# Two more input pairs transposed on VectorE in a matmul with rotary embedding

## The chip, the cores and the metric

The kernel runs on one core of a Trainium2 chip. The metric is the device time of one execution, in microseconds (us), as the median of several runs.

The core has five engines with a queue of instructions each: TensorE (PE in the profile; its weight loads are PEld), VectorE (DVE), ScalarE (ACT), GpSimd (POOL) and SyncE (SP). They run beside one another and wait for each other through semaphores. Here SP issues nearly all loads, ScalarE most stores, and GpSimd the loads of five pairs.

## The reference

```python
def reference(x, weight, cos, sin, n_heads):
    batch, seq, hidden = x.shape            # 16, 512, 768
    head_dim = hidden // n_heads            # 12 heads of 64
    y = np.matmul(x, weight)                # weight 768 x 768, all float32
    y = y.reshape(batch, seq, n_heads, head_dim)
    y1, y2 = y[..., :32], y[..., 32:]
    ...
    out1 = y1 * cos1 - y2 * sin1
    out2 = y2 * cos2 + y1 * sin2
    out = np.concatenate([out1, out2], axis=-1)
    return out.reshape(batch, seq, hidden)
```

So 8192 rows of 768 numbers are multiplied by one 768 x 768 matrix, and the result is rotated head by head with a cosine and a sine that depend on the row's place in its sequence.

## The kernel before

The 8192 rows are cut into 64 halves of 128 rows; two halves (`s` = 0 and 1, of two neighbouring batches) make a pair, `n` = 0 to 31. A pair goes through these stages:

1. Load. The 128 x 768 float32 rows of a half come to SBUF.
2. Cast to FP16 (`cast`, on ScalarE except at the start).
3. Transpose. A matmul contracts over the partitions, so the rows must be turned until the 768 columns lie on partitions, in six pieces of 128 x 128.
4. Matmul (`mm`, line 174): for each of the six pieces the transposed rows are the stationary operand, and 768 columns of the weight stream past.
5. `rope` (line 188) on VectorE: one instruction multiplies a PSUM bank with cosine and with sine into `tq`. `add` (line 199) on GpSimd adds the two products, crosswise, into `ov`.
6. `store` (line 244).

There are three ways through stages 1 to 3.

- An ordinary pair: two loads by SP, one for each half, into the ten buffers of `xpool` (`load`, line 83); casts on ScalarE; six TensorE transposes into PSUM for each half (`transpose`, line 140); and a copy out of PSUM on ScalarE (line 76).
- A pair in `BLOCKS` (8, 12, 16, 20, 24): four quarter loads by GpSimd, which cast on the way (`load_blocks`); no cast on ScalarE; one VectorE block transpose for each half (`transpose_blocks`, line 148).
- A pair in `BLOCKS_SP` (10, 14, 18, 22, 26): four quarter loads by SP in float32 into one of the two buffers of `hpool` (`load_blocks_sp`, line 99); two casts on ScalarE; one VectorE block transpose for each half.

VectorE's block transpose turns only blocks of 32 x 32 in place. That is why such a pair is loaded in quarters: each quarter puts 192 of the 768 columns of all rows on 32 of the partitions, so that the blocks, once turned, make up whole pieces.

The order on every engine is the order in which the program is written. The main loop runs over `n`. At its head it issues loads for later pairs: `load_pair(n + 5)`, and the four quarters of pairs `n + 8`, `n + 7`, `n + 6` and `n + 5`. Then for each half it does the matmuls, the transposes of the next pair (`upto("turn", ...)`), the casts of the pair after that (`upto("cast", ...)`), and the rope of one or two PSUM banks. The store of pair `n - 3` stands at the end. The last four pairs (`ALONE`) are handled in half banks of 384 columns, so that work left at the end is short. Pairs 0 to 6 are loaded ahead of the loop.

In the built program SP's and ScalarE's DMAs take eight completion semaphores in turn, and a DMA waits at its issuer until the DMA that used the same semaphore last has landed. A wait at the head of a queue holds up all that is queued behind it.

Of the kernel before, what the change touches and what calls it, by code (L numbers as in the profile page):

```python
# [17 lines left out]
def kernel(  # L18
# [23 lines left out]
    AHEAD = 7  # L42
    AHEAD_B = 8
    ALONE = 4
    BLOCKS = range(8, 25, 4)
    BLOCKS_SP = range(10, 27, 4)

# [30 lines left out]
    def load(n, s):  # L80
        b, r = where(n, s)
        xss[n, s] = xpool.tile([P, H], FP32, tag="xs", name="xs")
        nc.sync.dma_start(  # L83
            out=xss[n, s], in_=x[b].rearrange("(p r) h -> r p h", r=SB)[r]
        )

    def load_pair(n):
        for s in (0, 1):
            if n < NP and n not in BLOCKS and n not in BLOCKS_SP:
                load(n, s)  # L90
# [4 lines left out]
    def load_quarter(n, q, eng, dst):  # L95
        b, r = where(n, 0)
        src = x[b : b + 2].rearrange("b (j a r) (q k) -> r q a (b j) k", r=SB, a=R, q=NQ)
        dst = dst.rearrange("p s (j k) -> p (s j) k", j=NQ)
        eng.dma_start(out=dst[ts(q, R)], in_=src[r, q])  # L99

    def load_blocks(n, quarters):
        if n not in BLOCKS:
            return
        if quarters[0] == 0:
            xhs[n] = bpool.tile([P, 2, H], FP16, tag="xh", name="xh")
            x16[n, 0], x16[n, 1] = xhs[n][:, 0], xhs[n][:, 1]
        for q in quarters:
            load_quarter(n, q, nc.gpsimd, xhs[n])

    def load_blocks_sp(n, q):  # L110
        if n not in BLOCKS_SP:
            return
        if q == 0:
            xhs[n] = hpool.tile([P, 2, H], FP32, tag="xf", name="xf")
            xss[n, 0], xss[n, 1] = xhs[n][:, 0], xhs[n][:, 1]
        load_quarter(n, q, nc.sync, xhs[n])
# [11 lines left out]
    def cast(n, s, eng):  # L128
        xc = cpool.tile([P, H], FP16, tag="xc", name="xc")
        x16[n, s] = xc  # L130
        src = xss.pop((n, s))
        src = src.rearrange("p (m t e) -> p t m e", t=NT, e=2)
        copy(eng, xc.rearrange("p (t m e) -> p t m e", t=NT, e=2), src)
# [11 lines left out]
    def transpose_blocks(n, s):  # L145
        order = "p (j a t) -> p t j a" if n in BLOCKS else "p (t j a) -> p t j a"
        xT = tpool.tile([P, NT, P, 2], FP16, tag="xT", name="xT")
        nc.vector.transpose(  # L148
            out=xT.bitcast(FP32).rearrange("p t (j a) o -> p t j (a o)", j=NQ),
            in_=x16.pop((n, s)).bitcast(FP32).rearrange(order, j=NQ, t=NT),  # L150
        )
        xTT[n, s] = xT.rearrange("p t m e -> p t e m")
# [4 lines left out]
    def psum(n, s):  # L157
        key, banks = (n, 3) if n < NP - ALONE else ((n, s), 2)
        if key not in psys:
            psys[key] = [  # L160
                py_pool.tile([P, 512], FP32, tag="psy", name="psy") for _ in range(banks)
            ]
        ps = psys[key]
        if banks == 2:
            return [(ps[k][:, 0:HH], k * HH, (k + 1) * HH) for k in (0, 1)]
        cut = 512 if s == 0 else 256
        return [(ps[s][:, ds(s * 256, cut)], 0, cut), (ps[s + 1][:, 0 : H - cut], cut, H)]

    def mm(n, s, t, e, c0=0, c1=H):
        for k, (ps, lo, hi) in enumerate(psum(n, s)):  # L170
            a, z = max(c0, lo), min(c1, hi)
            if a >= z:
                continue
            nc.tensor.matmul(  # L174
                ps[:, a - lo : z - lo],
                xTT[n, s][:, t, e, :],
                w_sb[:, t, e, a:z],
                start=((t, e) == CHUNKS[0] and n > 1),
                stop=((t, e) == CHUNKS[-1] and (n > 1 or s >= k)),
            )  # L180
# [15 lines left out]
    def add(n, c0, c1, eng):  # L196
        w = c1 - c0
        tq = tqs[n][:, :, ds(c0, w)]
        eng.tensor_tensor(  # L199
            out=ovs[n][:, ds(c0, w)].rearrange("p (h t d) -> p h t d", t=2, d=HD),  # L200
            in0=tq[:, 0].rearrange("p (h t d) -> p h t d", t=2, d=HD),
            in1=tq[:, 1].rearrange("p (h t d) -> p h t d", t=2, d=HD)[:, :, ::-1, :],
            op=ADD,
        )

    def rope_bank(n, b):
        rope(n, b * 512, (b + 1) * 512, psys[n][b])

    def add_pair(n, step=2 * H):
        for c in range(0, 2 * H, step):  # L210
            add(n, c, c + step, nc.gpsimd)
# [8 lines left out]
    def rope_last(n, ps, c0, c1):  # L220
        nh = (c1 - c0) // D
        q = tqs[n][:, 1, c0:c1]
        ph = ps.rearrange("p (h d) -> p h d", d=D)
        for o, j in ((q.rearrange("p (h d) -> p h d", d=D), 1), (ph, 0)):
            nc.vector.tensor_tensor(  # L225
                out=o, in0=ph, op=MULT,
                in1=csn[:, j, n % SB, :].unsqueeze(1).broadcast_to((P, nh, D)),
            )
        nc.vector.tensor_tensor(  # L229
            out=ovs[n][:, c0:c1].rearrange("p (h t d) -> p h t d", t=2, d=HD),  # L230
            in0=ps.rearrange("p (h t d) -> p h t d", t=2, d=HD),
            in1=q.rearrange("p (h t d) -> p h t d", t=2, d=HD)[:, :, ::-1, :],
            op=ADD,
        )

    def store(n, eng, c0=0, c1=2 * H):
        b, r = where(n, 0)
        dst = out.rearrange("b (p r) h -> r p b h", r=SB)[r, :, b : b + 2]
        src = ovs[n].rearrange("p (b h) -> p b h", b=2)
        if c1 - c0 < 2 * H:  # L240
            s = c0 // H
            dst = dst[:, s, c0 - s * H : c1 - s * H]
            src = src[:, s, c0 - s * H : c1 - s * H]
        eng.dma_start(out=dst, in_=src)
# [32 lines left out]
        load_w(t, e)  # L277
    nc.sync.dma_start(out=csn[:, 0], in_=cos.rearrange("(p r) d -> p r d", r=SB))
    nc.sync.dma_start(out=sin_sb, in_=sin.rearrange("(p r) d -> p r d", r=SB))
    for n in range(2, AHEAD):  # L280
        load_pair(n)


    done = {"cast": 4, "turn": 4}

    def upto(what, k):
        while done[what] < min(k, 2 * NP):
            n, s = divmod(done[what], 2)
            done[what] += 1
            if what == "cast":  # L290
                if n not in BLOCKS:
                    cast(n, s, nc.scalar)
            elif n in BLOCKS or n in BLOCKS_SP:
                transpose_blocks(n, s)
            else:
                transpose(n, s, nc.scalar)
# [46 lines left out]
    for n in range(2, NP):  # L343
        load_pair(n + AHEAD - 2)
        for q, ahead in ((0, 8), (2, 7), (1, 6), (3, 5)):
            load_blocks_sp(n + ahead, q)
        for m, quarters in ((n + AHEAD_B, (0, 2)), (n + AHEAD_B - 1, (1, 3))):
            if m > BLOCKS[0]:
                load_blocks(m, quarters)
        for s in (0, 1):  # L350
            i = 2 * n + s
            if n < 4:

                for c0, c1 in ((0, 256), (256, H)):
                    for c in CHUNKS:
                        mm(n, s, *c, c0, c1)
                    if c0 == 0:
                        upto("turn", i + 2)
                        upto("cast", i + 4)
            elif n < NP - ALONE:  # L360
                for c in CHUNKS:
                    mm(n, s, *c)
            upto("turn", i + 3 if i > 6 else 0)
            upto("cast", i + 5 if i > 6 else 0)
            if n < NP - ALONE:
                for b in ((0,), (1, 2))[s]:
                    rope_bank(n, b)
                continue
            for ps, lo, hi in psum(n, s):
                for c in CHUNKS:  # L370
                    mm(n, s, *c, lo, hi)
                c0, c1 = s * H + lo, s * H + hi
                if (n, s, hi) == (NP - 1, 1, H):
                    rope_last(n, ps, c0, c1)
                    store(n, nc.sync, c0, c1)
                    continue
                rope(n, c0, c1, ps)
                add(n, c0, c1, nc.gpsimd)
                if (n, s) == (NP - 1, 1):
                    store(n, nc.scalar, c0, c1)  # L380
                elif hi == H:
                    store(n, nc.sync, s * H, (s + 1) * H)
        if n < NP - ALONE:
            if n >= 3:
                store(n - 3, nc.scalar)
            add_pair(n, H if n >= NP - ALONE - 2 else 2 * H)
        if n == NP - ALONE - 1:
            for m in (n - 2, n - 1, n):
                store(m, nc.sync)
# [34 lines left out]
```

## Time and profile before

| What | Value |
|---|---|
| Median of 4 runs | 155.12 us (154.9 to 155.26) |
| The profiled execution | 154.9 us; its span, first to last instruction, 152.8 us |
| Granted TensorE clock | 0.997 |
| TensorE busy | 146.1 us (96%) |
| VectorE busy | 130.1 us (85%) |
| GpSimd busy | 123.5 us (81%) |
| ScalarE busy | 76.6 us (50%) |
| TensorE transposes (L140) | 264 |
| VectorE block transposes (L148) | 10 of pairs loaded by GpSimd, 10 of pairs loaded by SP |
| DMA | 51.17 MB, mean 335 GB/s over the span |

"Busy" is the time in which an engine had an instruction running. For TensorE it overstates, since matmuls overlap. The chain that ended last is the page's better guide: it follows the last instruction back, at each step to the one that released it. Times in the trace count from the start of the span. A group's row gives busy time and mean duration, and after the second bar the idle time of the engine just before them. A row of a DMA gives the size and the median time from issue to landing.

### The profile page before, as it was taken

To read this page: it belongs to the slowest core of one execution; us is meant where nothing else is said; L and a number is where in the kernel's file an instruction comes from. 1 tells how busy PE (TensorE), PEld (TensorE's weight loads), DVE (VectorE), ACT (ScalarE), POOL (GpSimd) and SP (SyncE) were. 2 spreads that over 40 slices of the span, in tenths; PEclk is the share of its full clock that TensorE was granted. 3 is DMA by queue.
4 is the path that set the end of the run, shared out by engine and by line. 5 is a ranking of instruction groups with operands and counts; after the bars stand their busy time and mean duration, and the time that the engine had idled before them with its cause. 6 is when DMAs were issued, how large, how long until landed. Compare 5 with 4: busy or idle time off the path is not lost.

```text
span 152.8 us, 2768 instructions
## 1 busy us (share of the span) xinstructions
PE 146.1 (96%) x1062; PEld 93.0 (61%) x1062; DVE 130.1 (85%) x136; ACT 76.6 (50%) x95; POOL 123.5 (81%) x72
## 2 busy tenths in 40 slices
PE   6999999999999999999999999999999999999970
PEld 2455777666656666666666566666656666666640
DVE  0657999777798999989898989989898987987991
ACT  3440696868444826182525726255616548876200
POOL 1000399999997999799997999787897879899990
PEclk9999999999999999999999999999999999999998
DMA  4999999999999999999999999999999927896555
GB/s 153 369 394 403 402 380 321 244 350 380 317 338 404 356 327 350 347 373 404 323 321 375 406 351 294 309 405 407 409 413 412 406 94 303 327 365 246 206 206 206
DMA packets 27437, 51.17 MB, mean 335 GB/s; under 512 B 7200, under 2 KB 12960, under 8 KB 27424
## 3 DMA queue, kind: packets, MB, share of 16 engines
q1 hardware_dynamic: 15040, 29.17, 54.3%
q10 hardware_dynamic: 6944, 19.86, 33.0%
q0 software_dynamic: 5440, 1.97, 10.5%
q8 instruction: 8, 0.13, 0.3%
q14 instruction: 5, 0.04, 0.1%
HBM read 27.79 MB, written 25.17 MB: 347 GB/s over the span
## 4 chain that ended last, share of the span: by engine, by line
PE 86%; DMA 4%; DVE 4%; SPq 2%; issue 1%; DVEq 0%
PE psy L174 77%; PE pt L140 9%; DMA w_raw<-in_weight_dram 4%; DVE tq L188 3%; SPq L123 1%; SPq L83 1%; DVE w_sb L126 0%; DVE psy L225 0%; DVE ov L229 0%; DVE tq L225 0%; DVEq L229 0%; DVEq L188 0%
## 5 line engine op out<-in xcount | busy, mean ns | idle before, releaser
L174 PE MATMUL psy<-w_sb,xT 128*128 128x256 f16 (+2 forms) x781 | 132.0, 323 | 0.4 <-DVE w_sb L126 0.2
L188 DVE TENSOR_TENSOR tq<-psy,csn 128x1024 f32<-128x1024 f32 (+1 forms) x99 | 112.0, 1171 | 12.1 <-PE psy L174 11.4
L199 POOL TENSOR_TENSOR ov<-tq 128x1536 f32<-128x1536 f32 (+2 forms) x45 | 111.4, 2499 | 8.8 <-DVE tq L188 4.6
L174 PEld LDWEIGHTS <-xT 128*128 128x128 f16 x781 | 74.6, 98 | 44.9 <-issue 0.6
L76 ACT COPY xT<-pt 128x768 f16<-128x768 f16 x42 | 33.5, 797 | 54.8 <-PE pt L140 54.7
L76 ACT CAST xc<-xs 128x768 f16<-128x768 f32 x42 | 36.8, 906 | 10.9 <-DMA xs<-in_x_dram 8.1
L140 PE MATMUL pt<-ident,xc 128*128 128x128 f16 x264 | 21.8, 219 | 0.3 <-DVE xc L78 0.3
L140 PEld LDWEIGHTS <-xc 128*128 128x128 f16 x264 | 18.3, 98 | 6.2 <-DVE xc L78 1.1
L329 POOL COPY mark<-xs 128x1 f32<-128x1 f32 x1 | 0.2, 183 | 15.8 <-DMA xs<-in_x_dram 15.8
L99 POOL DMA_DIRECT2D xh<-in_x_dram x20 | 11.8, 593 | 0.5 <-issue 0.5
L76 ACT CAST xc<-xf 128x768 f16<-128x768 f32 x10 | 9.1, 910 | 0.0
L254 PE MATMUL psy<-cold 128*128 128x512 f16 x17 | 6.2, 510 | 1.2 <-DVE cold L261 1.2
L148 DVE STREAM_TRANSPOSE xT<-xh 128x384 f32<-128x384 f32 x10 | 7.0, 703 | 0.0
L148 DVE STREAM_TRANSPOSE xT<-xc 128x384 f32<-128x384 f32 x10 | 5.6, 564 | 0.0
L126 DVE CAST w_sb<-w_raw 128x768 f16<-128x768 f32 (+2 forms) x7 | 3.5, 502 | 2.2 <-DMA w_raw<-in_weight_dram 2.2
L78 DVE CAST xc<-xs 128x768 f16<-128x768 f32 x2 | 1.9, 953 | 2.8 <-DMA xs<-in_x_dram 2.8
L254 PEld LDWEIGHTS <-cold 128*128 128x128 f16 x17 | 1.9, 125 | 3.5 <-issue 2.2
L78 DVE COPY xT<-pt 128x768 f16<-128x768 f16 x2 | 1.1, 558 | 1.5 <-PE pt L140 1.5
L76 ACT ACT_TABLE_LOAD x1 | 1.3, 1283 | 0.7 <-PEq L405 0.7
L261 DVE MEMSET cold<- 128x256 uint32 x1 | 0.3, 272 | 0.9 <-PEq L405 0.9
L229 DVE TENSOR_TENSOR ov<-psy,tq 128x384 f32<-128x384 f32 x1 | 0.6, 557 | 0.0
L225 DVE TENSOR_TENSOR tq<-psy,csn 128x384 f32<-128x384 f32 x1 | 0.6, 558 | 0.0
(9 smaller groups left out, 1.9 us busy)
## 6 DMA issues: line engine op xcount, KB each, us to landing
out_dram<-ov ACTq DMA_DIRECT2D x25, 768.0 KB, 8.4
xs<-in_x_dram SPq DMA_DIRECT2D x44, 384.0 KB, 9.4
xf<-in_x_dram SPq DMA_DIRECT2D x20, 192.0 KB, 11.5
out_dram<-ov SPq DMA_DIRECT2D x7, 384.0 KB, 2.4
out_dram<-ov SPq DMA_DIRECT2D x3, 768.0 KB, 4.8
w_raw<-in_weight_dram SPq DMA_DIRECT2D x5, 384.0 KB, 6.9
xh<-in_x_dram POOLq DMA_DIRECT2D x20, 96.0 KB, 9.9
w_raw<-in_weight_dram SPq DMA_DIRECT2D x1, 256.0 KB, 5.5
```

Source lines behind the costliest of these rows:

```text
L76: eng.copy(out=o, in_=i_)
L78: eng.tensor_copy(out=o, in_=i_)
L83: nc.sync.dma_start(out=xss[n, s], in_=x[b].rearrange("(p r) h -> r p h", r=SB)[r])
L99: eng.dma_start(out=dst[ts(q, R)], in_=src[r, q])
L123: nc.sync.dma_start(out=w_raw[t, e][:, c0:c1], in_=wv[t, e, :, c0:c1])
L126: nc.vector.tensor_copy(out=w_sb[:, t, e, c0:c1], in_=w_raw[t, e][:, c0:c1])
L140: nc.tensor.transpose(pt[:, t, e, :], xc[:, t, e, :], ident)
L148: nc.vector.transpose(out=xT.bitcast(FP32).rearrange("p t (j a) o -> p t j (a o)", j=NQ), in_=x16.pop((n, s)).bitcast(FP32).rearrange(orde ...
L174: nc.tensor.matmul(ps[:, a - lo : z - lo], xTT[n, s][:, t, e, :], w_sb[:, t, e, a:z], start=((t, e) == CHUNKS[0] and n > 1), stop=((t, e) ...
L188: nc.vector.tensor_tensor(out=tqs[n][:, :, c0:c1].rearrange("p j (h d) -> p j h d", d=D), in0=ps.rearrange("p (h d) -> p h d", d=D) .unsqu ...
L199: eng.tensor_tensor(out=ovs[n][:, ds(c0, w)].rearrange("p (h t d) -> p h t d", t=2, d=HD), in0=tq[:, 0].rearrange("p (h t d) -> p h t d", ...
L254: nc.tensor.matmul(psys[n][b], cold[:, 0:P], cold, start=True, stop=opened[0] < WARM - 6)
```

## The change

Pair 6 and pair 28 move from the ordinary way to that of `BLOCKS_SP`. Pair 6 is then loaded ahead of the loop in four quarters, in the place where its two loads were. Pair 28's quarters are issued in the loop at `n` = 20 to 23, where before its two loads stood at `n` = 23. Pair 28 comes two pairs after pair 26, while other pairs of this kind are four apart, and `hpool` still has two buffers.

```diff
-    BLOCKS_SP = range(10, 27, 4)
+    BLOCKS_SP = (*range(6, 27, 4), 28)
...
-    for n in range(2, AHEAD):
+    for n in range(2, AHEAD - 1):
         load_pair(n)
+    for q in (0, 2, 1, 3):
+        load_blocks_sp(AHEAD - 1, q)
...
         for q, ahead in ((0, 8), (2, 7), (1, 6), (3, 5)):
-            load_blocks_sp(n + ahead, q)
+            if n + ahead >= AHEAD:
+                load_blocks_sp(n + ahead, q)
```

`AHEAD` is 7. On the engines, by the order of the built programs: TensorE loses 24 transposes with their weight loads, ScalarE four copies out of PSUM, VectorE gains four block transposes (pair 6's stand among pair 5's products, pair 28's among pair 27's), and SP has four DMAs more. GpSimd's instructions stay as they are.

## The prediction

> **What bounds the kernel now.** I read the busy rows and the summary of the chain on the page first, then the chain in order of time, then the groups, windows and timeline at the places the edit touches.
>
> ```profile
> PE   6999999999999999999999999999999999999970
> DVE  0657999777798999989898989989898987987991
> POOL 1000399999997999799997999787897879899990
> PEclk9999999999999999999999999999999999999998
> ...
> PE 86%; DMA 4%; DVE 4%; SPq 2%; issue 1%; DVEq 0%
> ```
>
> TensorE shows 9 in every slice from the second to the third from the end, at full granted clock, and holds 86% of the chain that ended last. VectorE and GpSimd are close behind. The chain in order of time shows what TensorE does without a break from 12.05 us to 143.2:
>
> ```profile
> 33.96 0.34 PE pt L140 x6
> 34.29 1.95 PE psy L174 x12
> 36.24 0.34 PE pt L140 x6
> ...
> 41.15 5.85 PE psy L174 x36
> ...
> 142.18 0.99 PE psy L174 x6
> 143.19 0.96 DVE tq L188
> ```
>
> A half pair costs 1.95 us of matmuls (12 pieces), and each half pair transposed on TensorE adds a group of six transposes of 0.335 us (0.34 rounded). The two groups shown at 33.96 and 36.24 are pair 6's: pairs 4 and 5 end just before them, and the long run from 41.15 is where pair 8, a block pair, needs none. So a pair costs 4.57 us with TensorE transposes and 3.90 without. In the middle two pairs take 8.47 us. VectorE there:
>
> ```profile
> core 0: us, PE busy (x) PEld busy (x) DVE busy (x) ACT busy (x) POOL busy (x), PEclk, DMA share, GB/s
> 47.30:64.30 17.00, 17.00 (x123) 10.79 (x121) 15.94 (x17) 8.03 (x10) 16.03 (x8) 1.00 1.10 353
> ```
>
> Four pairs take 17 us and leave VectorE about 1 us and GpSimd about 1 us: balanced, but TensorE leads.
>
> **The change part by part.** TensorE: 24 transposes (two pairs, two halves, six pieces) and their weight loads go, four groups of 0.335 us = -1.34 us, all on the chain. ScalarE: four copies out of PSUM go (4 x 0.80 = -3.2 us); it is half idle, so nothing. Four casts read xf in place of xs, 0.91 us for 0.91. VectorE gains four block transposes:
>
> ```profile
> L148 DVE STREAM_TRANSPOSE xT<-xc 128x384 f32<-128x384 f32 x10 | 5.6, 564 | 0.0
> L76 ACT CAST xc<-xf 128x768 f16<-128x768 f32 x10 | 9.1, 910 | 0.0
> ```
>
> In the timeline the next VectorE instruction starts 0.49 us after one, so 4 x 0.49 = 1.96 us. Whether they lie beside TensorE's work is decided per place. Pair 6: its transposes run during pair 5's matmuls, in a stage where VectorE waits 0.88 us for TensorE in each 4.57 us pair. Pair 5 then takes TensorE 3.90 us and VectorE 3 x 1.15 + 0.98 = 4.43, but pairs 4 and 6 give back 1.1 us each. Cost 0, gain 0.67 us. Pair 28: its transposes run during pair 27. By the starts in the trace, VectorE reaches the last product of pair 26 at 126.47 - 0.67 = 125.80; then first transpose 126.97, product 127.46, second transpose 128.57, pair 27's second product 129.05. TensorE would let that product start at 129.90 - 1.005 = 128.90. So VectorE is 0.15 late there, and at pair 28's first product (131.35 against 130.2) 1.1 late. TensorE does not feel it: its PSUM banks come free 2.6 us before pair 29 writes them (131.4 against 134.0). Pairs 28 to 30 cost TensorE 2.29 us per half and VectorE 1.93, so the lag is gone by pair 29's second half. The full 1.34 us is in place before the last pair.
>
> GpSimd at the end is the tighter one:
>
> ```profile
> 131.26 17.99 POOL L199 TENSOR_TENSOR ov<-tq 128x768 f32<-128x768 f32 x17 [0.57 <-POOL ov L199]
> ```
>
> 17 additions run back to back from pair 27's first half to 149.25. They start when pair 27's second product is done (131.12), which in the new order is 130.27: 0.85 earlier, not 1.34. Their end moves to 148.4. The last store behind GpSimd then lands at 151.20 - 0.85 = 150.35, and the one behind VectorE at 151.72 - 1.34 = 150.38. Just level: the gain stays 1.34, with no reserve. If GpSimd lost its lead there, the cover is gone and the gain is 0.85.
>
> A rule of the Trainium skill speaks against this step. SBUF — State Buffer, section "SBUF: two separate sides", says that VectorE in a two-port mode and GpSimd take a shared port pair as an exclusive lock for a whole instruction. The trace:
>
> ```profile
> 81.58 3.47 POOL L199 TENSOR_TENSOR ov<-tq 128x1536 f32<-128x1536 f32 x1 [0.89 <-POOL ov L199]
> ...
> 86.17 3.47 POOL L199 TENSOR_TENSOR ov<-tq 128x1536 f32<-128x1536 f32 x1
> 86.86 0.56 DVE L148 STREAM_TRANSPOSE xT<-xc 128x384 f32<-128x384 f32 x1
> ```
>
> The first addition has no block transpose beside it, the second has one inside it, and both take 3.47 us. By the lock, pair 28's two transposes would push GpSimd's last additions by 2 x 0.56 = 1.1 us, and the gain of 0.85 would become a loss of 0.3. By the rows it is 0; I take the rows.
>
> **Loads and their queue.** Two pairs change from two loads of 384 KB to four of 192 KB, so SP issues four more DMAs (about 0.33 us each, while SP mostly waits).
>
> ```profile
> xs<-in_x_dram SPq DMA_DIRECT2D x44, 384.0 KB, 9.4
> xf<-in_x_dram SPq DMA_DIRECT2D x20, 192.0 KB, 11.5
> ...
> 8.53 9.91 SPq L83 DMA_DIRECT2D xs<-in_x_dram  x12
> ...
> 30.45 0.90 ACT L76 CAST xc<-xs 128x768 f16<-128x768 f32 x1
> ...
> 32.04 0.80 ACT L76 COPY xT<-pt 128x768 f16<-128x768 f16 x1 [0.69 <-PE pt L140]
> ```
>
> In the built program's list of waits SP and ScalarE share eight completion semaphores, and a DMA waits until the previous one with its semaphore has landed. At the start these give one issue per 0.97 us. Pair 6's quarters take the issue times of pairs 6 and 7 in the kernel before: 15.2, 16.1, 17.1, 18.1. With the 11.5 us of the row the last lands at 29.6; the full-size load issued at 18.1 landed at 29.3. The cast at 30.45 needs all four quarters, and ScalarE may start it as late as 32.2 before TensorE waits (its copy is needed at 33.96). So it fits, by 1 to 2.5 us. [...] The row says 11.5 with the queues full; I keep the row, and with it the risk. What a late load costs: from 0 to the 2 us by which 13.9 us, the slowest landing of a quarter in the trace, would pass it here. A gain is excluded, since the old cast did not wait for its data. I take 0, as the load issued at the same time arrived.
>
> Everything behind pair 6 on SP is later by two loads. Pair 7's issue moves from 17.1 and 18.1 to about 20 and 22; it lands near 32 and is cast at 33.8. Pair 11 gets the semaphore of ScalarE's second store, so it is issued near 40 and not 31, and lands near 50, where its cast would start at 50.5; TensorE needs it at 54.8. Pair 28's first quarter waits for pair 22's second cast (101.5), since its two buffers are two blocks deep and pair 26 holds the other; behind it on SP wait pair 26's last quarters and pairs 27 to 31. Those of 26 land near 111 and are cast at 115. Its own last quarter waits for a store issued near 102, and lands near 120 for a cast at 123.7. GpSimd's own loads keep their places. All covered, by 3 us or more.
>
> **Sum.** -0.67 - 0.67 = -1.34 us of 154.9, the time of the profiled execution (span 152.8 and 2.1 around it): 153.56. The median of the runs, 155.12, is 0.22 above it: 153.8.
>
> **The rivals.** (1) GpSimd's end decides, or small waits eat part: gain 0.4 to 0.85, 154.3 to 154.7. For it: additions without a gap to the end. Against: by 0.03 us the other store is last. (2) Slower: ScalarE's store blocks its copies. A store issued by ScalarE waits for its semaphore too, and whatever is queued behind it waits along. Most exposed is pair 14's store (84.3 before, 83.6 after): its semaphore's previous user becomes pair 22's third quarter. That one follows, semaphore by semaphore, pair 5's store (49.2), pair 18's first quarter (57.6) and pair 19's first half (68 to 69), so it is issued near 79 and lands at 90.5 with 11.5 us. Behind the store waits the copy of pair 19's transposes, which must start by 90.45 or TensorE idles (matmuls at 91.3, copy 0.8). From that point each us of lateness is a us lost. With the slowest landing, 13.9 us, it is 2.5 us: net +1.1, 156.2. For it: the margin is nil by medians, and VectorE has no spare to catch up. Against: fewer loads are queued at 79 than before, and in the kernel before the store at 104.4 held the next casts back by 2.8 us (102.1 to 104.9) and TensorE did not wait. (3) Such a wait of about 1.3 us cancels the gain: 155.1.
>
> **How the numbers follow.** Full gain 0.58, part gain 0.12, nothing 0.09, slower 0.21. About 0.2%, 0.3 us, is what a measurement of this kernel can tell from none. Faster by more: 0.70; within: 0.09; slower: 0.21. The range runs from 153.5 (full gain and the runs' spread of 0.2) to 155.7, taking in part gain, none, and the mildest losses; what lies above is half of the slower case.
>
> **What would show it.** Right: 240 transposes at L140; the runs of matmuls from pair 5 to pair 6 unbroken; the matmuls 0.67 us earlier than before from 36 us on and 1.34 earlier from 131 on; GpSimd's last series starting near 130.4. Wrong: idle time of TensorE's matmuls on "ACT xT", above all near 91 or 33; VectorE's product waiting 1 us or more; a store of ScalarE that stands for several us. If TensorE shows idle time beyond 1 us in the middle, the forecast fails.

## The result, and the profile after

| | Before | After |
|---|---|---|
| Median | 155.28 us (154.9 to 156.09, 64 runs) | 155.18 us (154.32 to 156.59, 43 runs) |
| Profiled execution | 154.9 us, span 152.8 | 154.54 us, span 152.4 |

The ratio is 0.9997, with a 95% interval from 0.9986 to 1.0008: no change. The forecast of 153.8 us is missed, though the measured time lies in its range. One thing in the table is more than a zero: after's runs scatter over 2.3 us, before's over 1.2. A ratio leaves out runs that lie over 1.5% above the fastest of their kernel: none here, further down one of e1's and nine of e8's.

The page of after first, in the rows that were read before the change:

```profile
PE   6989999999999999999999999999999999999950
DVE  0666999779898989989898989989898989997890
POOL 1000399999998999799997999787888879999990
PEclk9999999999999999999999999999999999999999
...
PE 85%; DMA 5%; DVE 4%; SPq 2%; issue 1%; DVEq 0%
...
L140 PE MATMUL pt<-ident,xc 128*128 128x128 f16 x240 | 19.9, 219 | 0.3 <-DVE xc L78 0.3
...
L148 DVE STREAM_TRANSPOSE xT<-xc 128x384 f32<-128x384 f32 x14 | 7.9, 564 | 0.0
...
xs<-in_x_dram SPq DMA_DIRECT2D x40, 384.0 KB, 9.1
xf<-in_x_dram SPq DMA_DIRECT2D x28, 192.0 KB, 10.4
```

The edit did what it says: 240 transposes on TensorE instead of 264, four more block transposes on VectorE, eight quarter loads for four full ones. TensorE still shows 9 from the fourth slice to the third from the end and has 85% of the chain, against 86%. Nothing on the page says why the time stood still. The chain in order of time shows TensorE's gain arriving:

```profile
12.27 4.45 PE psy L174 x26
...
31.90 0.34 PE pt L140 x6
32.23 5.85 PE psy L174 x36
38.08 0.33 PE pt L140 x6
...
141.06 0.99 PE psy L174 x6
...
142.08 0.96 DVE tq L188
```

The run of 36 matmuls at 32.23 holds those of pair 6, with no transposes between them any more. The stream began 0.22 us later than before (12.27 against 12.05, when the first weights had landed), and its last piece starts at 141.06 against 142.18. So TensorE is 1.12 us ahead at the end, and 1.34 ahead from its own start: exactly four groups of 0.335. VectorE follows it: its last instruction ends 1.12 us earlier, at 148.57 against 149.69. Then more than half of it is lost. The timeline at the end, first of after, then of before:

```profile
130.57 18.00 POOL L199 TENSOR_TENSOR ov<-tq 128x768 f32<-128x768 f32 x17 [0.31 <-POOL ov L199]
...
148.02 0.56 DVE L229 TENSOR_TENSOR ov<-psy,tq 128x384 f32<-128x384 f32 x1
148.59 0.38 ACTq L244 DMA_DIRECT2D out_dram<-ov  x1
148.60 0.33 SPq L244 DMA_DIRECT2D out_dram<-ov  x1
```

```profile
149.13 0.56 DVE L229 TENSOR_TENSOR ov<-psy,tq 128x384 f32<-128x384 f32 x1
149.28 0.35 ACTq L244 DMA_DIRECT2D out_dram<-ov  x1
149.71 0.33 SPq L244 DMA_DIRECT2D out_dram<-ov  x1
```

GpSimd's last series now ends at 148.56, together with VectorE, and the last two stores are issued together: ScalarE's (behind GpSimd) at 148.59, SP's (behind VectorE) at 148.60. Before, ScalarE's went out 0.43 us ahead of SP's (149.28 and 149.71). The list of DMAs in the last stretch gives the time from issue to landing, first for after, then for before:

```profile
out_dram<-ov ACTq DMA_DIRECT2D x1, 192.0 KB, 2.5
out_dram<-ov SPq DMA_DIRECT2D x1, 192.0 KB, 2.2
```

```profile
out_dram<-ov ACTq DMA_DIRECT2D x1, 192.0 KB, 1.9
out_dram<-ov SPq DMA_DIRECT2D x1, 192.0 KB, 2.0
```

Issued together they take 2.46 and 2.19 us, apart 1.92 and 2.01. So the last landing moves only from 151.72 to 151.05, 0.67 us, and it is now ScalarE's store. Behind it SP goes through the eight completion semaphores one by one, in a fixed order, about 0.06 us each. In before the last store was on the sixth of the eight, and SP was done 0.21 us after the landing; in after it is on the first, all the others come behind it, and SP is done 0.51 us after. The list of SP's waits shows it as one wait in after (the first row) where before there were three short ones (the second):

```profile
SPq L422 <- DMA out_dram<-ov: 2.0, 1, 2.0
```

```profile
SPq L419 <- DMA out_dram<-ov: 1.3, 3, 0.5
```

For these two executions the books close: 1.34 us gained on TensorE, less 0.22 at the start, less 0.45 because the stores coincide, less 0.30 in the last waits, is 0.37 us, and the span fell by 0.37.

Without the later start, which is chance (e4 below, the same kernel, starts earlier than before), that would be a gain of 0.6 us, but the medians show 0.1. The prediction named the place where the rest could go: ScalarE near 90 us. ScalarE's timeline in the profiled execution of after:

```profile
84.64 1.69 ACT L76 CAST xc<-xs 128x768 f16<-128x768 f32 x2
89.43 0.38 ACTq L244 DMA_DIRECT2D out_dram<-ov  x1
89.91 0.80 ACT L76 COPY xT<-pt 128x768 f16<-128x768 f16 x1 [3.57 <-DMA xf<-in_x_dram]
```

The store of pair 14 stands at the head of ScalarE's queue from the end of the casts (86.3) to 89.43, until a quarter of pair 22 has landed (issued at 77.08, landed at 89.35, 12.3 us). ScalarE is idle for 3.57 us before the copy of pair 19's transposes. Most of that it would have waited for the transposes themselves (their row starts at 88.74; without a store in the way the copy follows 0.59 us after that, as e3 shows below); the store adds about 0.6. TensorE's next matmuls, at 91.36, need the copy, which ends at 90.71: in this execution it passes with some 0.6 us to spare. One profile can't say how often it does not.

### The profile page after: what moved, and what is told of

Its sections match the earlier page's. It is cut to its first block, busy times and chain, and to the rows that moved or that the text cites. A ratio compares the mean times of both kernels' runs of the same rounds, so it can differ in the third digit from the quotient of the medians.

```text
span 152.4 us, 2721 instructions
## 1 busy us (share of the span) xinstructions
PE 144.9 (95%) x1038; PEld 91.7 (60%) x1038; DVE 131.3 (86%) x140; ACT 73.6 (48%) x91; POOL 123.6 (81%) x72
## 3 DMA queue, kind: packets, MB, share of 16 engines
q0 software_dynamic: 5440, 1.97, 10.7%
## 4 chain that ended last, share of the span: by engine, by line
PE 85%; DMA 5%; DVE 4%; SPq 2%; issue 1%; DVEq 0%
PE psy L174 77%; PE pt L140 8%; DMA w_raw<-in_weight_dram 5%; DVE tq L188 3%; SPq L123 1%; SPq L83 1%; DVE w_sb L126 0%; DVE psy L225 0%; DVE ov L229 0%; DVEq L229 0%; DVE tq L225 0%; DVEq L188 0%
## 5 line engine op out<-in xcount | busy, mean ns | idle before, releaser
L76 ACT COPY xT<-pt 128x768 f16<-128x768 f16 x38 | 30.3, 798 | 58.0 <-PE pt L140 54.4
L76 ACT CAST xc<-xs 128x768 f16<-128x768 f32 x38 | 33.0, 905 | 9.6 <-DMA xs<-in_x_dram 8.6
L140 PE MATMUL pt<-ident,xc 128*128 128x128 f16 x240 | 19.9, 219 | 0.3 <-DVE xc L78 0.3
L140 PEld LDWEIGHTS <-xc 128*128 128x128 f16 x240 | 16.7, 98 | 5.8 <-DVE xc L78 1.1
L76 ACT CAST xc<-xf 128x768 f16<-128x768 f32 x14 | 12.6, 903 | 0.0
L148 DVE STREAM_TRANSPOSE xT<-xc 128x384 f32<-128x384 f32 x14 | 7.9, 564 | 0.0
```

Of the source, the lines that this page charges most:

```text
L76: eng.copy(out=o, in_=i_)
L140: nc.tensor.transpose(pt[:, t, e, :], xc[:, t, e, :], ident)
L148: nc.vector.transpose(out=xT.bitcast(FP32).rearrange("p t (j a) o -> p t j (a o)", j=NQ), in_=x16.pop((n, s)).bitcast(FP32).rearrange(orde ...
```

## The experiments

Two theories. **S, the stall**: in most executions that store is later than in the profiled one and TensorE idles near 91 us. **E, the end**: GpSimd's last series, the coinciding stores and the order of SP's last waits take back about 0.7 us in every execution.

The table holds all kernels that were run; e5, e6 and e10 have six timed runs each, e7 four. "Span" is the median span of the timed runs less that of the kernel before in the same session; "outside" is the median of time less span (2.14 or 2.15 us for before); "tail" is taken from the profile: from the start of GpSimd's last series (130.57 in the fence above) to the end of the span. For after, the span of before in its session is worked out from the median, 155.28 less 2.15. A run's span is on record to 0.1 us, so a difference of 0.1 in that column says nothing. In brackets stand the values without the runs that the ratio leaves out.

| Run | Median us | Ratio to before, 95% | Span | Outside | Tail |
|---|---|---|---|---|---|
| before | 155.12 to 155.42 | 1 | 0 | 2.15 | 21.5 |
| after | 155.18 | 0.9997 [0.9986, 1.0008] | -0.1 | 2.14 | 21.8 |
| e4, after again | 154.79 | 0.9983 [0.9967, 0.9998] | -0.35 | 2.14 | 21.8 |
| e1, pair 6 alone | 155.05 (154.85) | 1.0001 [0.9975, 1.0027] | +0.1 (0) | 2.05 | 21.4 |
| e2, pair 28 alone | 154.74 | 0.9968 [0.9955, 0.998] | -0.1 | 1.87 | 21.4 |
| e3, after, one load cut | 154.46 | 0.9964 [0.995, 0.9977] | -0.7 | 2.17 | 21.8 |
| e5, e3 and one addition on VectorE | 154.03 | 0.9912 [0.9896, 0.9928] | -1.2 | 1.93 | 21.2 |
| e6, e3 and another order of stores | 154.43 | 0.9944 [0.9926, 0.9962] | -1.0 | 2.13 | 21.5 |
| e7, e3 and both | 153.64 | 0.989 [0.9873, 0.9907] | -1.55 | 1.88 | 20.9 |
| e8, after, two loads cut | 155.97 (154.99) | 0.9975 [0.9954, 0.9995] | +0.7 (-0.3) | 2.02 | 21.7 |
| e9, before with the end's edits | 155.55 | 1.0014 [1.0004, 1.0025] | +0.5 | 1.98 | not unbroken |
| e10, e2 and one addition on VectorE | 154.09 | 0.9925 [0.9908, 0.9942] | -0.8 | 1.79 | 20.9 |

**e1_only6 and e2_only28: each pair alone.** e1 is after without pair 28, e2 is before with it:

```diff
-    BLOCKS_SP = (*range(6, 27, 4), 28)
+    BLOCKS_SP = range(6, 27, 4)           # e1_only6
```
```diff
-    BLOCKS_SP = range(10, 27, 4)
+    BLOCKS_SP = (*range(10, 27, 4), 28)   # e2_only28
```

> Pair 6 alone joins; pair 28 stays ordinary. Theory S (a store of ScalarE stalls TensorE in most executions: pair 14's store waits for pair 22's third quarter, landed at 89.34 us in the profile after, and holds the copy of pair 19's transposes, which must start by about 90.7): the exposed chain of semaphores is the same here, so 0.67 us less TensorE work is partly eaten, median 154.8 to 155.3 and runs as scattered as after (over 1.5 us from fastest to slowest). Theory E (TensorE's gain arrives in full, and it is lost at the end: GpSimd's last series 0.43 us, last waits on semaphores 0.31 us): GpSimd's series shifts by the whole 0.67 and the last two stores have semaphores at the end of SP's list of waits (0.13 shorter), so 154.4 to 154.5, runs as close as before.

> Pair 28 alone joins; pair 6 stays ordinary. Theory S: pair 14's store follows a store here, as in the kernel before, so nothing stalls; runs as close as before (about 1 us from fastest to slowest). Both theories: TensorE gains 0.67 us, GpSimd's last series starts only 0.2 earlier, so the end gains 0.2 to 0.4 (with 0.13 from the last semaphores): 154.8 to 155.0.

Measured: e1 scatters as after does (154.33 to 156.42, and one run at 158.74) and gains nothing; e2 is narrow (154.17 to 154.92) and has no gap on TensorE. ScalarE's timeline of e1 has the store a whole microsecond later than after's profile had it, and TensorE's has a gap behind it, and a second one 18 us later:

```profile
90.53 0.38 ACTq L244 DMA_DIRECT2D out_dram<-ov  x1
91.00 1.50 ACT L76 COPY xT<-pt 128x768 f16<-128x768 f16 x2 [4.85 <-PE psy L174]
```

```profile
91.86 3.42 PE L174 MATMUL psy<-w_sb,xT 128*128 128x512 f16 x20 [0.71 <-ACT xT L76]
...
109.44 1.80 PE L174 MATMUL psy<-w_sb,xT 128*128 128x512 f16 x10 [0.37 <-ACT xT L76]
```

(The copies' row names another releaser, but they start right behind the store, with their own transposes long done.) The second gap is of the same kind: a store of ScalarE at 108.11, whose semaphore's previous user, a load, landed at 108.04, with a copy behind it. In after and e4 that store meets another DMA, and there is no gap.

So in these runs the stall comes with pair 6, whose quarters shift all later DMAs by two places in the turn of the eight semaphores. Pair 28 alone does not bring it. Its own gain needs care: of its 0.47 us (before had 155.21 in that session) only 0.1 lies in the span by the medians (0.26 by the profiles, 152.50 against 152.76), and 0.28 lie outside it, in time that the trace does not show. The 0.67 us of its two groups are in the span only where the end lets them be, as e10 shows below.

**e4_again: the kernel after, unchanged**, for a second profile.

> The change itself again, for a second profile and for its runs beside the others on one chip. Theory S: where the time is above 154.6, TensorE shows idle time of as much near 91.5 us, with ScalarE's copy of pair 19 later than 90.7. Theory E: no idle time of TensorE, whatever the time; the difference lies behind 142 us.

This profile caught the stall. TensorE's timeline, and then the chain in order of time:

```profile
90.53 0.50 PE L140 MATMUL pt<-ident,xc 128*128 128x128 f16 x6
91.86 3.42 PE L174 MATMUL psy<-w_sb,xT 128*128 128x512 f16 x20 [0.84 <-ACT xT L76]
```

```profile
78.42 12.04 DMA xf<-in_x_dram
...
90.53 0.38 ACTq L244
...
91.01 0.81 ACT xT L76
...
91.86 2.23 PE psy L174 x13
```

This is the blocking in one column: the quarter takes 12.04 us and lands at 90.46, the store is issued at 90.53, the copy starts at 91.01 and ends at 91.82, the matmuls start at 91.86. TensorE stood for 0.84 us with the transposes of that copy long done. Store and copy have no data in common with that quarter; the semaphore alone ties them. The whole loss is a little more than the row's 0.84: at pair 4 this execution was 0.50 us ahead of after's (transposes at 25.04 against 25.54), at its last transposes 0.51 behind (141.08 against 140.57), 1.01 us in all. That earlier start is why the two times, 154.54 without the stall and 155.06 with it, differ by only 0.52. The scatter of after's runs did not come back here: e4's lie within 0.83 us (154.51 to 155.34), so scatter alone is no proof of the stall.

**e3_split23: move the tie.** One load of 384 KB, the first of pair 23, is cut in two. Its data, its place and the work are the same; it only takes one semaphore more, so that pair 14's store falls on the semaphore of an earlier store (pair 12's), which lands well before the copy is due. All later ties move by one too; none of them stops TensorE in e3's profile.

```diff
-        nc.sync.dma_start(
-            out=xss[n, s], in_=x[b].rearrange("(p r) h -> r p h", r=SB)[r]
-        )
+        src = x[b].rearrange("(p r) h -> r p h", r=SB)[r]
+        cuts = (0, 384, H) if (n, s) == (23, 0) else (0, H)
+        for c0, c1 in zip(cuts, cuts[1:]):
+            nc.sync.dma_start(out=xss[n, s][:, c0:c1], in_=src[:, c0:c1])
```

> The change, with the load of pair 23's first half cut in two by columns: one DMA more, so that pair 14's store takes the semaphore of pair 12's store (landed 87.7 in the profile after) and no longer that of pair 22's third quarter. Theory S: the stall goes, median 154.4 to 154.6, and the runs stay within about 1 us. Theory E: nothing but the last waits changes (0.06 us shorter): 155.1, runs as scattered as after.

ScalarE's timeline has the store 2.5 us earlier, right behind the landing of pair 12's (86.81), and the copy waits for nothing but its transposes, whose row starts at 88.54:

```profile
86.88 0.38 ACTq L245 DMA_DIRECT2D out_dram<-ov  x1
...
89.13 0.80 ACT L76 COPY xT<-pt 128x768 f16<-128x768 f16 x1 [2.40 <-PE pt L141]
```

The runs lie within 153.9 to 154.94, and the ratio's interval lies wholly below after's. The median span is 0.6 us below that of after's first measurement and 0.35 below e4's, each against before. Of that 0.06 belongs to the end, where e3's last landing is on the second semaphore of SP's row and no longer on the first; the rest, 0.3 to 0.55, is what S costs in the typical run. (The intervals of e3 and e4 overlap, so by the times of one session S is not proven; the profiles, with 0 and 0.84 us of idle time, settle it.) But e3 gains 0.7 us in the span and not 1.34. S is only half of it.

**e8_split2: the tie once more, later.** With both loads of pair 23 cut, the turn moves by two, and the store falls on pair 22's fourth quarter, which is issued after the third.

```diff
-        cuts = (0, 384, H) if (n, s) == (23, 0) else (0, H)
+        cuts = (0, 384, H) if n == 23 else (0, H)
```

> The change, with both loads of pair 23 cut in two: two DMAs more, so that pair 14's store takes the semaphore of pair 22's fourth quarter, which landed 1.9 us after the third in the profile after (91.20 against 89.34). Theory S (what counts is which DMA the store has to wait for): the stall is longer, TensorE idles about 1 us or more near 91.5, time 155.3 to 156.5, though one DMA more than in e3 is all that differs. Rival (e3 gained because its halved load was faster, or by chance): as e3, 154.5.

TensorE's timeline of e8:

```profile
91.16 0.50 PE L141 MATMUL pt<-ident,xc 128*128 128x128 f16 x6
93.22 2.01 PE L175 MATMUL psy<-w_sb,xT 128*128 128x512 f16 x11 [1.56 <-ACT xT L76]
```

The quarter lands at 91.81, the store is issued at 91.89, and TensorE idles for 1.56 us instead of 0.84, in an execution of 156.03 us. One more cut gives no stall, the next a worse one: neither the load itself nor its size matters, but whose semaphore the store meets. This rests on the profile. The times alone do not carry it: the runs go from 153.92 to 158.82, but over those that the ratio counts e8 can't be told from e3. What the longest of them lost, no profile shows.

**e5_relief, e6_rotate, e7_both: the end.** All three start from e3, where no stall disturbs. e5 takes the last addition of pair 29 from GpSimd to VectorE. e6 writes the results of pairs 28 and 29 and of the first half of pair 30 out in two stores for each half and not one; the further DMAs move the turn on, so that the last stores fall late in SP's row of waits. e7 does both.

```diff
-                add(n, c0, c1, nc.gpsimd)
+                add(n, c0, c1, nc.vector if (n, s, hi) == (29, 1, H) else nc.gpsimd)   # e5, e7
```
```diff
+                elif (n, s) < (30, 1):            # e6, e7
+                    store(n, nc.sync, c0, c1)
                 elif hi == H:
```

> e3_split23, and VectorE does one of GpSimd's last additions (the second half bank of pair 29's second half). Theory E (with the stall gone, GpSimd's last series still ends the program: 17 additions back to back, its store lands at 150.85 us, 0.25 after VectorE's): GpSimd gains 0.96 us on a lag of 0.4, its store goes out earlier and alone, and the end comes 0.3 to 0.5 us sooner than in e3: 154.0 to 154.2. Rival (the end is set by TensorE and VectorE alone): nothing, 154.5, or 0.5 worse, for VectorE has one instruction more.

> e3_split23, and five of the last stores on SP are cut in two, so that the two stores that end the program take the last two of the eight semaphores and not the second and third. Theory E (at the end SP waits for the eight semaphores one by one in a fixed order, about 0.06 us each, so that a last store with an early semaphore leaves 6 waits to go through behind it): 0.25 to 0.3 us sooner than e3, 154.2, with SP's last instruction 0.1 to 0.2 us after the last landing and not 0.45. Rival (the order costs nothing): 154.5, or later by the five more issues of 0.33 us if these delay SP.

> e3_split23 with both edits, e5's and e6's. If the two losses at the end are separate, they add up: 0.5 to 0.8 us sooner than e3, 153.7 to 153.9, ratio to the kernel before 0.991 to 0.993.

The timeline of e7:

```profile
130.70 17.49 POOL L200 TENSOR_TENSOR ov<-tq 128x768 f32<-128x768 f32 x16 [0.32 <-POOL ov L200]
...
139.61 0.88 DVE L200 TENSOR_TENSOR ov<-tq 128x384 f32<-128x384 f32 x1
...
148.15 0.56 DVE L230 TENSOR_TENSOR ov<-psy,tq 128x384 f32<-128x384 f32 x1
148.22 0.35 ACTq L245 DMA_DIRECT2D out_dram<-ov  x1
```

VectorE does the one addition at 139.61 in 0.88 us; GpSimd is done 17.49 us after the start of its series and not 18.00, and ScalarE's store goes out 0.5 us ahead of VectorE's end again. The relief is half of an addition and not a whole one, for VectorE's addition is not free to GpSimd: GpSimd's next one, which starts beside it, takes 1.34 us where the others take 1.00 (timeline of e7):

```profile
140.02 1.34 POOL L200 TENSOR_TENSOR ov<-tq 128x384 f32<-128x384 f32 x1
```

In e5 the two stores then take 1.94 and 1.97 us and not 2.46 and 2.21, the tail falls from 21.8 to 21.2, and the ratio's interval lies wholly below e3's. e6 changes the other term: SP is done 0.14 us after the last landing, in e3 0.45. By times alone e6 and e3 can't be told apart (their intervals overlap, and the 154.2 that was expected did not come); by the profile its tail is 0.3 shorter (21.77 to 21.45), and its span of -1.0 against -0.7 agrees. In e7 SP is done 0.08 us after the last landing. Its list of waits has the row of after, now split and short:

```profile
SPq L425 <- DMA out_dram<-ov: 1.0, 2, 0.5
```

With both, the tail is 20.9 and the time 153.64 us, 0.989 of before. It is the best of all kernels, though its interval overlaps e5's. E holds by the profiles, and its two terms add up: 0.5 and 0.3 us.

**e9_before_end: the end's edits without the change**, on the kernel before (with the stores of pair 28 alone cut).

```diff
-                add(n, c0, c1, nc.gpsimd)
+                add(n, c0, c1, nc.vector if (n, s, hi) == (29, 1, H) else nc.gpsimd)
...
+                elif (n, s) < (29, 0):
+                    store(n, nc.sync, c0, c1)
```

> The kernel before, without pairs 6 and 28 changed, with both edits at the end (VectorE takes one of GpSimd's last additions; two of SP's last stores are cut so that the final two take the last two semaphores). Theory E (these losses at the end are what the change brings, for in the kernel before GpSimd's store went out 0.43 us ahead of VectorE's and its last store had the sixth of eight semaphores): 0.1 to 0.2 us sooner, ratio 0.999. Rival (the end edits are a gain of their own, and e7 owes them most): ratio 0.993 to 0.996, as e7 against e3.

Measured: 0.2 us slower, where 0.1 to 0.2 faster was expected. So e7's gain is not that of the end's edits by themselves. The timeline of e9 shows why they did harm here:

```profile
141.11 1.42 DVE L199 TENSOR_TENSOR ov<-tq 128x384 f32<-128x384 f32 x1
...
143.48 2.91 POOL L199 TENSOR_TENSOR ov<-tq 128x384 f32<-128x384 f32 x3 [1.36 <-DVE tq L188]
```

VectorE's addition starts just behind one of GpSimd's (141.10 to 142.12) and takes 1.42 us, not 0.88; GpSimd then waits 1.36 us for the product behind it. So GpSimd, with one addition less, ends level with VectorE (both at 150.22) where before it ended 0.43 us ahead, and the two stores are issued 0.01 us apart and take 2.45 and 2.18 us. Brought about by another edit, the coincidence of the stores costs the same as in after. (The whole execution is also 0.5 us later than before's from the first weights on.)

**e10_only28_end: pair 28 with e5's edit, without pair 6.**

```diff
-    BLOCKS_SP = range(10, 27, 4)
+    BLOCKS_SP = (*range(10, 27, 4), 28)
...
-                add(n, c0, c1, nc.gpsimd)
+                add(n, c0, c1, nc.vector if (n, s, hi) == (29, 1, H) else nc.gpsimd)
```

> Pair 28 alone, as e2, with VectorE taking one of GpSimd's last additions (its last stores have the last two semaphores already). If each pair brings 0.67 us of TensorE and GpSimd's series hid most of pair 28's: 0.67 plus 0.13 for the semaphores, 154.3 to 154.5, ratio 0.995, that is 0.2 to 0.3 below e2. If pair 28 costs VectorE something that shows: no better than e2, 154.7.

Measured: 1.2 us faster in the time, 0.8 in the span. The span is what pair 28's 0.67 us come to once the end lets them through, with 0.12 from the last store's place, now the eighth of SP's row (SP is done 0.09 us after the landing, in before 0.21). The other 0.35 us lie outside the span: 1.79 us there against 2.15. Why some kernels have less time there (e2, e5, e7 and e10) no row of the trace shows, and it stays open. It also means that 0.2 to 0.3 us of what e5 and e7 gain in the time is not E's, and it is part of why e2, e7 and e10 came in below what was expected.

## Why the prediction was wrong, step by step

- **TensorE's 1.34 us: right.** The stream is 1.34 us ahead of before, counted from its own start, and 240 transposes are left.
- **VectorE's block transposes hidden: right.** VectorE's end moved by as much as TensorE's last piece, 1.12 us in the profiles.
- **GpSimd and the shared port: right to take the rows.** Pair 28's block transposes ran at 127.16 and 128.76, inside three additions of GpSimd that took 7.03 us from 123.23; the same three took 7.02 before, with no block transpose beside them. The lock that the Trainium skill describes (SBUF — State Buffer, "SBUF: two separate sides") would have added 1.1 if it held for them; nothing of that shows here. The section speaks of VectorE in a two-port mode or with two inputs in SBUF, and no run tells that a block transpose is such a case, so the prediction was right not to charge for it, but the row does not speak against the rule. VectorE's addition in e9, which has two inputs in SBUF, did take longer beside GpSimd's (1.42 us, against 0.88 in e7).
- **Pair 6's quarters: off by 1 us, without cost.** The last landed at 30.59, not 29.6, and its cast started at 30.68, within the 32.2 allowed. TensorE's stream has no gap there.
- **The step that failed: the sum has no term for ScalarE's blocked store.** "I take 0" was said of pair 6's load, and there it was right. For the store the sum is silent, though rival 2 had worked out its landing (90.5) against its limit (90.45). It called that margin nil, and it was less than nil: what lies between that landing and the start of the copy was left out, 0.56 us in after (89.35 to 89.91) and 0.55 in e4 (90.46 to 91.01), of which the issue of the store itself takes 0.38. With it, rival 2's own figures give a stall of 0.6 us in the median, and the likeliest cost was not 0. The profiles have the landing at 89.35 in one execution and at 90.46 in the next, for an idle time of 0 and of 0.84 us, and the typical run loses 0.3 to 0.55. The mechanism, the place and the chain of semaphores were rival 2's; its price of 2.5 us, for the slowest landing, was too high for the typical run, and it did not turn the sign. The argument against it, that a store at 104.4 held casts back by 2.8 us without TensorE waiting, spoke of another place with a margin of its own.
- **The term mis-sized: "Just level: the gain stays 1.34".** GpSimd's end came 0.91 us earlier from the stream's start, even better than the 0.85 taken, and VectorE's 1.34. So the two ends met as predicted. But the landings were taken from stores issued 0.43 us apart. Issued together they take 2.46 and 2.19 us, where 1.92 and 2.01 were carried over: 0.45 us of the gain. And the time behind the last landing was taken as fixed, while it depends on which of the eight semaphores the last store has: another 0.30. Together 0.75, so that an execution without a stall gains 0.6 (e3: 0.7 in the span, 0.06 of it by its semaphore). This loss is in every execution and is the larger of the two. The prediction had 0.85 as the gain "if GpSimd lost its lead"; the lead was lost by becoming nil.
- **The sum as it stands now:** 1.34, less 0.75 at the end, less 0.3 to 0.55 near 91 us, is 0.05 to 0.3 us. Measured: 0.1 (after) and 0.35 to 0.4 (e4). The last term comes from these same medians, so the sum is not a test of it; the 0.75 is read from the profiles. What was called rival 3, a wait that cancels the gain, is what happened, in two pieces and not in one.

## What to carry to other kernels

Where DMAs of several engines take completion semaphores in turn, every DMA added or removed changes which earlier transfer each later one waits for: list the pairs anew, and look for a slow load ahead of an engine's store with that engine's other work behind it. Count into the margin what lies between a landing and the work that waits for it (here 0.55 us, most of it the store's own issue), and cost a margin of nil as a likely stall, not as nothing. When a chain is shortened, follow the gain to the very last wait of the kernel: here more than half of it was lost behind the last arithmetic instruction, and one addition moved and one order of stores changed brought it back.

## What the runs showed of the hardware

- The last two stores of 192 KB, issued by two engines within 0.02 us of each other, took 2.44 to 2.47 and 2.16 to 2.22 us to land in all seven profiles where they coincide (after, e2, e3, e4, e6, e8, e9); issued 0.43 to 0.52 us apart they took 1.91 to 2.02 in all five others.
- The same quarter load of 192 KB in the same kernel took 12.3 us in one execution and 12.0 in another (issued at 77.08 and 78.42). A landing 1.1 us later, 90.46 and not 89.35, made the difference between no idle time and 0.84 us.
- The waits at the end cost about 0.06 us for each semaphore that is still to be passed: 0.51 us from the last landing to SP's end with the last store on the first of the eight (after), 0.45 on the second (e3), 0.21 on the sixth (before) and 0.08 on the eighth (e7).
- One addition of 128x384 float32 moved to VectorE took 0.88 us there in e7 and 1.42 in e9, and the addition that GpSimd started beside it in e7 took 1.34 us against 1.00. That the two hold each other up is what these times suggest; no run tests it alone.
- The time outside the span was 2.15 us for before and 1.79 to 1.93 for four of the kernels. No row tells what sets it.
